# Weight products of a hybrid encoder layer: 512 columns and two token groups at a time, in place of 256 columns and one

## The chip, the cores and the metric

The kernel runs on one core of one Trainium2 chip. The metric is the device time of one launch in microseconds (us). The core's engines are named as in the profile: PE is the matrix engine and PEld its load of the stationary operand, DVE the vector engine, ACT the scalar engine, POOL the GpSimd engine, SP the engine that issues most transfers. L321 is line 321 of the kernel.

## The reference

One encoder layer for two sequences, `x_prompt` of 512 tokens (g = 0 in the kernel) and `x_sample` of 1024 tokens (g = 1), width 1024, all in float32. Gated linear attention with eight heads (A) and retention with eight heads (R) run side by side over the same projection `u @ w_in`; their outputs are mixed by gates and go through the last product, `w_out`.

```python
ada = jax.nn.silu(c) @ w_ada + b_ada
shift, scale, gate = jnp.split(ada, 3, axis=-1)
u = x * (1 + scale[:, None, :]) + shift[:, None, :]
proj = u @ w_in                                       # [T, 7168 + 1024]
aq, af_f, af_b, ai, ag, rq, rk, rv, rg = jnp.split(proj, IN_OFFSETS, axis=-1)
...
o_a = _hgrn2_dir(q_a, k_f, logf_f, v_a) + _flip(_hgrn2_dir(...))
y_a = (_rms_norm(o_a) * a_norm_w).reshape(B_, T, A_WV) * jax.nn.silu(ag.astype(F32))
q_r = _apply_rope(rq ..., cos, sin) * R_DK ** -0.5
k_r = _apply_rope(rk ..., cos, sin)
o_r = _layer_norm(_retention_dir(q_r, k_r, v_r, lg[0]) + _flip(_retention_dir(...)))
y_r = (o_r.reshape(B_, T, R_WV) * jax.nn.silu(rg.astype(F32))).astype(dt)
p_a = y_a @ w_pa
p_r = y_r @ w_pb
g_a, g_r = jnp.split(jax.nn.sigmoid(u @ w_mg + b_mg), 2, axis=-1)
s = (g_a * p_a + g_r * p_r) @ w_out
h = DEEPNORM_ALPHA * x + (1 + gate[:, None, :]) * s
return (_layer_norm(h) * ln_g + ln_b).astype(dt)
```

## The kernel before

**Products.** Every large product is exact: both operands are split into a high and a low F32R part, and three matmuls per slice of 128 of the contraction (high by low, low by high, high by high) are added up in a PSUM bank. `gemm_f` holds weight columns stationary and moves 512 tokens (L310). `gemm_t` holds 128 tokens stationary and moves 256 weight columns (L321); its outputs have tokens on the partitions. Both are generators: they yield after every 12 matmuls of 256 columns, or 6 of 512.

**Weights.** `Stream` holds the weights in their order of use. A piece of 512 KB is loaded into one of two raw buffers, ACT writes its high part (L94), DVE its low part (L103; POOL in the last product of g = 0), and both stand in a ring of four slots until the product has used them. A piece of 128 columns takes one slot; for `gemm_t` two pieces take two slots and give 256 columns.

**Banks.** The large products share three PSUM banks (`gbank`, tile name `g`), the attention stages have three others (`l`) and two (`t`). A bank is free for its next use when ACT or DVE has read the last result out of it. Two token groups of 256 columns fill one bank, and their read-out (the evacuation) is emitted behind the second.

**Order.** The program is scheduled by hand: the order in which the code emits instructions is each engine's order. `interleave` (L129) draws on a generator of matmuls, the filler, and at each yield emits, where they are due, the split of the next weight piece and attention stages (`Stage`); the code behind a yield, such as an evacuation, follows behind them. The sequence g = 0 has units A0 to A3, then R0 and R1, each of two heads (lanes). While the stages of a unit run, the filler is `mid` of the same unit (A: values and output gates; R: values, then gates) and `pre` of the next (A: queries and forget gates by `gemm_f`; R: queries and keys, rotated). Then come the gate products and blocks of 512 tokens (one for g = 0, two for g = 1, which are the last two), each with `pblock` (`w_pa`, `w_pb`, by `gemm_f`) and `oblock` (`w_out`, by `gemm_t`). In `oblock`, `epi` (L933) evacuates a bank (L937), adds the residual (L940) and takes statistics (L941); `finish` (L911) normalises a row of 128 tokens and stores it. In the last block, it is emitted right behind the last `epi` of its row. While `oblock` of g = 0 runs, stages transpose and scale the tokens of g = 1 (L1004, L1009, L1015).

```python
while i < len(stages):
    ...
    th = s.w * max(left + credit, 0.0) / max(weight, 1e-9)
    if credit < th:
        break
    ...
    s.fn()
```

The functions that the diff touches, with their lines:

Of the kernel before, what the change touches and what calls it, by code (L numbers as in the profile page):

```python
# [25 lines left out]
class Stream:  # L26
    """The weights in order of use: raw pieces are loaded, split into two F32R parts, used, released."""
# [28 lines left out]
    def open(self, j):  # L56
        """the slots of a piece, if they are free"""
        kind, ps = self.todo[j]
        need = 2 if kind == "t" else 1
        if self.used + need > self.ring:  # L60
            return False
        self.used += need
        if kind == "t":
            h = self.w_pool.tile([128, NK, 256], F32R, name="wh", tag="w", bufs=self.ring)
            l = self.w_pool.tile([128, NK, 256], F32R, name="wl", tag="w", bufs=self.ring)
            self.tiles[j] = (h, l)
            self.parts = [(h[:, :, 128 * i:128 * i + 128], l[:, :, 128 * i:128 * i + 128]) for i in range(2)]
        else:
            shape = [128, 2, 768] if kind == "k" else [128, 2, NK, 128]
# [59 lines left out]
def interleave(filler, total, stages, marks, ws, lead=0.0):  # L129
    """Emit the filler's steps with the stages spread between them, after a lead, and the weights' splits."""  # L130
# [32 lines left out]
def layer(ctx, tc, x_p, x_s, c_p, c_s, w_ada, b_ada, w_in, hgrn_lb, a_norm_w, ret_decay, w_pa, w_pb, w_mg, b_mg,  # L163
# [86 lines left out]
    def order_pre(u):  # L250
        if u.kind == "A":
            for ls in u.wl:
                h = u.lanes[ls[0]][0]
                for seg in range(3):
                    ws.add("f", (w_in, 1024 * seg + 128 * h))
        else:
# [4 lines left out]
    def order_mid(u):  # L261
        if u.kind == "A":
# [16 lines left out]
    for g in range(2):  # L279
# [15 lines left out]
        for b in range(NT[g] // 512):  # L295
            for part, n in p_order:
                ws.add("f", ((w_pa, w_pb)[part], 128 * n))
            for n in range(4):
                ws.add("t", (w_out, 256 * n), (w_out, 256 * n + 128))
# [5 lines left out]
    def gemm_f(ps, w, a):  # L305
        """ps[n, t] += sum_k w[k, n] a[k, t]; a: (hi, lo) as lists of [128, 512] over k"""
# [9 lines left out]
    def gemm_t(ps, w, a, t0, k0=0, k1=NK):  # L316
        """ps[t, n] += sum_k a[k, t] w[k, n]"""
# [9 lines left out]

    def u_f(g, b):
# [49 lines left out]

    def mid_A(u):
# [26 lines left out]
    def update(u, l, h):  # L406
        """decays of blocks of h become those of blocks of 2h"""
# [174 lines left out]
    def pre_R(u):  # L582
        u.X, u.Vt, u.Gt, u.St, u.C = {}, {}, {}, {}, {}
        for ls in u.wl:
            j, w = ws.get()
            for l in ls:
                b = u.lanes[l][1]
                X = u.X[l] = sb("X", [128, 4, 384])
                for c in range(0, 4, 2):
# [3 lines left out]
                    for e in range(2):  # L593
                        r = 4 * b + c + e
                        t = sb("sg", [128, 2, 256])
                        a = ps[:, e, 0:1]
                        sw = bass.AP(a.tensor, a.offset + 32, [list(a.ap[0]), [64, 4], [-32, 2], [1, 32]])
                        cos = rope[:, r, 0:1, :].to_broadcast([128, 4, 64])
                        sin = rope[:, r, 1:2, :].rearrange("p o (a b) -> p o a b", a=2).to_broadcast([128, 4, 2, 32])
                        V.tensor_tensor(out=t[:, 0, :].rearrange("p (a b) -> p a b", a=4),  # L600
                                        in0=ps[:, e, :].rearrange("p (a b) -> p a b", a=4), in1=cos, op=ALU.mult)
                        V.tensor_tensor(out=t[:, 1, :].rearrange("p (a b c) -> p a b c", a=4, b=2), in0=sw, in1=sin,
                                        op=ALU.mult)
                        tq = [t[:, i, 0:128].rearrange("p (a o b) -> p a o b", a=2, o=1).to_broadcast([128, 2, 2, 64])
                              for i in range(2)]
                        G.tensor_tensor(out=X[:, c + e, 0:256].rearrange("p (a o b) -> p a o b", a=2, o=2),
                                        in0=tq[0], in1=tq[1], op=ALU.add)
                        G.tensor_tensor(out=X[:, c + e, 256:384], in0=t[:, 0, 128:256], in1=t[:, 1, 128:256],
                                        op=ALU.add)
# [231 lines left out]
    yb = {}  # L841

    def load_y(g, b, part):
        """the loads of a part's two halves, in four pieces"""
# [61 lines left out]
    def oblock(g, b, st, last):  # L906
        hs, gt, lg, lb = st["h"], bc["gt"], bc["lg"], bc["lb"]
        ap_s = [lambda k, t0, p=p: st["s"][k // 4][p][:, k % 4, t0:t0 + 128] for p in range(2)]
        stat = cp.tile([128, 4, 28], F32, name="stat", tag="stat")

        def finish(i):  # L911
            def fn():
                h, ss = hs[i], stat[:, i]
                V.bn_aggr(ss[:, 24:26], ss[:, 0:24].rearrange("p (a b) -> p a b", a=4))  # L914
                G.tensor_scalar(out=ss[:, 26:27], in0=ss[:, 25:26], scalar1=EPS, scalar2=None, op0=ALU.add)  # L915
                G.tensor_tensor(out=ss[:, 27:28], in0=ss[:, 26:27], in1=nhalf[:, 0:1], op=ALU.pow)
                for q in range(2):
                    hq = h[:, 512 * q:512 * q + 512]
                    V.scalar_tensor_tensor(out=hq, in0=hq, scalar=ss[:, 24:25], in1=lg[q], op0=ALU.subtract,
                                           op1=ALU.mult)  # L920
                t0 = 512 * b + 128 * i
                for q in range(2):
                    hq = h[:, 512 * q:512 * q + 512]
                    if q == 0 or (last and i == 3):
                        V.scalar_tensor_tensor(out=hq, in0=hq, scalar=ss[:, 27:28], in1=lb[q], op0=ALU.mult,
                                               op1=ALU.add)
                    else:
                        S.activation(out=hq, in_=hq, func=AF.Copy, scale=ss[:, 27:28])
# [4 lines left out]
        def epi(n, i, ps):  # L933
            m = ps.shape[1]
            t = sb("sg", [128, m, 256])
            gg = gt[n // 2][:, 256 * (n % 2):256 * (n % 2) + 256].rearrange("p (o c) -> p o c", o=1)
            V.tensor_tensor(out=t, in0=ps, in1=gg.to_broadcast([128, m, 256]), op=ALU.mult)  # L937
            for e in range(m):
                h = hs[i + e][:, 256 * n:256 * n + 256]
                V.scalar_tensor_tensor(out=h, in0=h, scalar=ALPHA, in1=t[:, e, :], op0=ALU.mult, op1=ALU.add)  # L940
                V.bn_stats(stat[:, i + e, 6 * n:6 * n + 6], h)  # L941

        ws_n = {}

        def part(n, i, step, left):
            if n not in ws_n:
                ws_n[n] = ws.get()
            j, w = ws_n[n]
            ps = gbank([128, step, 256])
            for e in range(step):  # L950
                yield from gemm_t(ps[:, e, :], w, ap_s, 128 * (i + e))
            epi(n, i, ps)
            if not left:
                ws.done(j)

        # the last rows of s come last
        ws_n[0] = ws.get()
        banks = [gbank([128, 1, 256]) for _ in range(2)]
        for k0, k1 in ((0, NK - 1), (NK - 1, NK)):
            for e in range(2):  # L960
                yield from gemm_t(banks[e][:, 0, :], ws_n[0][1], ap_s, 128 * e, k0, k1)
        for e in range(2):
            epi(0, e, banks[e])
        order = [(0, 2, 1), (0, 3, 1), (1, 0, 2), (1, 2, 2), (2, 0, 2)]
        if last:
            order += [(3, 0, 1), (3, 1, 1), (2, 2, 1), (3, 2, 1), (2, 3, 1), (3, 3, 1)]
        else:
            order += [(2, 2, 2), (3, 0, 2), (3, 2, 2)]
        for x, (n, i, step) in enumerate(order):
            yield from part(n, i, step, any(m == n for m, _, _ in order[x + 1:]))  # L970
            if last and n == 3:
                finish(i)()
        st["finish"] = [] if last else [Stage(finish(i)) for i in range(4)]

# [44 lines left out]
    def u_parts():  # L1019
        """the next part of each product of u_stage that still lacks one"""  # L1020
# [6 lines left out]
    def ada_mm(ps, w):  # L1027
        """silu(c) times columns of w_ada: four sums over k, rows 32 j and 32 j + 1 of ps"""
# [4 lines left out]
    def ada_out(ps, row, jobs):  # L1033
        """the sum of the four, with the columns on the partitions, plus a bias and a constant"""
# [6 lines left out]
    def startup():  # L1041
# [47 lines left out]
        # silu(c) = c / (1 + exp(-c))  # L1089
# [12 lines left out]
        def bounds():  # L1102
# [3 lines left out]
            # softmax over the one layer, its cumulative sum less its first row  # L1106
# [11 lines left out]
        def log_sigmoids():  # L1118
            # lg = log_sigmoid(r) = min(r, 0) - log1p(e), e = exp(-|r|); log1p(e) = 2 atanh(z), z = e / (2 + e)
# [107 lines left out]
    def pre(u):  # L1227
        return pre_A(u) if u.kind == "A" else pre_R(u)

    def mid(u):  # L1230
        return mid_A(u) if u.kind == "A" else mid_R(u)
# [96 lines left out]
```

## Time and profile before

| | |
|---|---|
| time, median of 3 runs | 2136.13 us (2135.5 to 2137.14) |
| span of the profiled execution, first to last instruction | 2135.2 us |
| mean granted clock of the matrix engine in it | 0.998 of full speed |
| PE busy | 2108.5 us, 99% of the span |
| DVE, ACT, POOL busy | 53%, 35%, 20% |
| chain that ended last: PE's share | 95% |
| of it `gemm_f` (L310) and `gemm_t` (L321) | 41% and 38% |

The profile is of one execution; what lies around its span is 0.9 us to the median of the runs. The chain that ended last is followed back from the last instruction, at each step to what released it. Matrix products are pipelined, and the end of one is modelled, so that the time of a run of them is read from their starts, not from the length of one.

### The profile page before, as it was taken

Reading aid. Unit: us, or ns where it says so; the run is one execution under the profiler, and the core shown is the slowest. Engines: PE = TensorE matmul, PEld = TensorE weight load, DVE = VectorE, ACT = ScalarE, POOL = GpSimd, SP = SyncE. Lnnn points to the kernel's source line nnn. Section 1 sums busy time; section 2 is a strip of 40 time slices with the busy share of each in tenths; the row PEclk is TensorE's granted clock in tenths of the full one; section 3 lists DMA queues with packets and bytes.
Section 4 is the critical chain, followed back from the end, with each engine's and each line's share of the span. In section 5 each row is a group of like instructions: output and inputs, shape, how many; then the busy total and the mean of one; then the engine's idle time right before and its main releaser. Section 6 shows DMA issues by size and latency. Waiting matters only on the chain.

```text
span 2135.2 us, 45792 instructions
## 1 busy us (share of the span) xinstructions
PE 2108.5 (99%) x19331; PEld 1892.8 (89%) x19331; DVE 1122.3 (53%) x2242; ACT 746.7 (35%) x1570; POOL 437.7 (20%) x668
## 2 busy tenths in 40 slices
PE   7999999999999999999999999999999999999997
PEld 5898899998888988899889889999999888889887
DVE  4856764644334965554565457353543442245657
ACT  3644553223322534444444435212121233322221
POOL 3322233321000332121121214332322100000101
PEclk9999999999999999999999999999999999999999
DMA  9322323246776421111111211212212256577752
GB/s 285 111 84 85 92 85 106 70 129 187 226 243 201 140 80 61 41 50 61 41 61 41 70 31 61 65 41 65 85 40 85 84 163 211 185 234 225 242 184 80
DMA packets 340205, 247.29 MB, mean 116 GB/s; under 512 B 9564, under 2 KB 303680, under 8 KB 338976
## 3 DMA queue, kind: packets, MB, share of 16 engines
q1 hardware_dynamic: 332112, 229.75, 34.9%
q10 hardware_dynamic: 6944, 12.59, 1.5%
q8 instruction: 152, 2.49, 0.5%
q0 software_dynamic: 944, 2.02, 0.3%
q14 instruction: 53, 0.43, 0.1%
HBM read 199.23 MB, written 45.10 MB: 114 GB/s over the span
## 4 chain that ended last, share of the span: by engine, by line
PE 95%; DMA 1%; DVE 1%; POOL 1%; issue 1%; ACT 1%; SPq 0%; POOLq 0%; DVEq 0%; ACTq 0%
PE g L310 41%; PE g L321 38%; PE l L542 2%; PE l L430 2%; PE t L505 2%; PE l L459 1%; PE l L742 1%; PE l L740 1%; PE t L677 1%; PE g L1171 1%; PE t L489 1%; PE l L1171 1%; PE t L707 1%; PE l L725 1%; PE t L1031 1%
## 5 line engine op out<-in xcount | busy, mean ns | idle before, releaser
L321 PE MATMUL g<-wh,u 128*128 128x256 f32 x3840 | 736.2, 287 | 0.0
L310 PE MATMUL g<-u,w 128*128 128x512 f32 x2736 | 671.7, 397 | 0.0
L321 PEld LDWEIGHTS g<-wh,u 128*128 128x128 f32 x3840 | 609.5, 191 | 8.9 <-issue 4.0
L310 PEld LDWEIGHTS g<-u,w 128*128 128x128 f32 x2736 | 499.7, 188 | 100.7 <-issue 1.2
L321 PE MATMUL g<-wl,u 128*128 128x256 f32 x1920 | 542.6, 283 | 0.0
L321 PEld LDWEIGHTS g<-wl,u 128*128 128x128 f32 x1920 | 367.1, 191 | 0.1
L103 DVE TENSOR_TENSOR w<-raw,w 128x1024 fp32r<-128x1024 f32 (+1 forms) x144 | 174.8, 1215 | 209.6 <-ACT w L94 209.5
L310 PE MATMUL g<-y,w 128*128 128x512 f32 x1152 | 261.8, 389 | 0.0
L310 PEld LDWEIGHTS g<-y,w 128*128 128x128 f32 x1152 | 216.1, 188 | 44.9
L414 DVE TENSOR_TENSOR X<-X,T 128x512 f32<-128x512 f32 x336 | 219.1, 698 | 22.2 <-issue 20.4
L94 ACT ACTIVATE w<-raw 128x1024 fp32r<-128x1024 f32 (+1 forms) x146 | 151.5, 1047 | 138.9 <-DMA raw<-in_w_pb 36.4
L103 DVE TENSOR_TENSOR wl<-raw,wh 128x1024 fp32r<-128x1024 f32 x98 | 122.6, 1262 | 104.2 <-ACT wh L94 104.2
L416 POOL TENSOR_TENSOR T<-T 128x512 f32<-128x512 f32 (+6 forms) x168 | 119.7, 739 | 83.6 <-DVE T L343 81.6
L94 ACT ACTIVATE wh<-raw 128x1024 fp32r<-128x1024 f32 x104 | 106.8, 1055 | 38.2 <-PE g L321 33.7
L321 PE MATMUL g<-wh,sl 128*128 128x256 f32 x384 | 109.0, 284 | 0.0
L446 POOL COPY A<-D 32x128 f32<-32x128 f32 x96 | 57.4, 598 | 248.4 <-DVE D L439 245.4
L321 PE MATMUL g<-wl,sh 128*128 128x256 f32 x384 | 107.6, 280 | 0.0
L321 PE MATMUL g<-wh,sh 128*128 128x256 f32 x384 | 107.6, 280 | 0.0
L403 ACT ACTIVATE KM<-X 128x256 f32<-128x256 f32 x120 | 51.5, 430 | 126.2 <-DVE X L414 122.5
L915 POOL TENSOR_SCALAR stat<-stat 128x1 f32<-128x1 f32 x12 | 9.2, 765 | 373.7 <-DVE stat L914 373.7
L826 ACT ACTIVATE sg<-g,vec 128x512 f32<-128x512 f32 x48 | 33.0, 687 | 127.2 <-PE g L310 127.2
L321 PEld LDWEIGHTS g<-wl,sh 128*128 128x128 f32 x384 | 73.3, 191 | 0.1
(197 smaller groups left out, 2390.7 us busy)
## 6 DMA issues: line engine op xcount, KB each, us to landing
raw<-in_w_in SPq DMA_DIRECT2D x122, 512.0 KB, 4.1
yd<-yT SPq DMA_DIRECT2D x96, 256.0 KB, 2.1
raw<-in_w_mg SPq DMA_DIRECT2D x48, 512.0 KB, 3.9
y<-yd SPq DMA_DIRECT2D x24, 1024.0 KB, 8.9
gd<-sg ACTq DMA_DIRECT2D x48, 256.0 KB, 2.7
raw<-in_w_pa SPq DMA_DIRECT2D x24, 512.0 KB, 4.7
raw<-in_w_pb SPq DMA_DIRECT2D x24, 512.0 KB, 4.0
gt<-gd SPq DMA_DIRECT2D x48, 256.0 KB, 4.7
```

Source lines behind the costliest of these rows:

```text
L94: self.nc.scalar.activation(out=hi, in_=raw, func=AF.Copy)
L103: self.lo.tensor_tensor(out=lo, in0=raw, in1=hi.bitcast(F32), op=ALU.subtract)
L310: T.matmul(ps, w[wi][:, k, :], a[ai](k), start=n == 0, stop=n == 3 * NK - 1)
L321: T.matmul(ps, a[ai](k, t0), w[wi][:, k, :], start=k == 0 and n == 0, stop=k == NK - 1 and ai == wi)
L403: S.activation(out=K4[:, :, 0, :], in_=halves(u.X[l][:, 0, :], h)[:, :, 0, :], func=AF.Copy)
L414: V.tensor_tensor(out=v, in0=v, in1=f, op=ALU.mult)
L416: G.tensor_tensor(out=T2, in0=Tv[:, :, :, 0], in1=Tv[:, :, :, 1], op=ALU.mult)
L430: T.matmul(ps[32 * i:32 * i + 32, c, :], km[:, c0:c0 + 32], qq, start=True, stop=True, tile_position=(0, 32 * i))
L446: G.tensor_copy(out=A[32 * i:32 * i + 32, :, 32 * i:32 * i + 32], in_=u.Dt[l][32 * i:32 * i + 32, :, :])
L505: T.matmul(ps[:, m, :], kt[:, m, :], u.Vt[l][:, c, :], start=True, stop=True)
L542: T.matmul(ps[:, c, :], a, b, start=i == 0, stop=i == len(mm) - 1)
L1171: T.matmul(acc[l, seg], w[wi][:, n0:n0 + 128], uh[0, 0, ai][:, k, :], start=k == 0 and n == 0, stop=k == 7 and n == 2)
```

## The change

Three products of g = 0 (`mid` of an A unit, `pre` and `mid` of an R unit) and `oblock` of all three blocks no longer use `gemm_t` but a new `gemm_q`. Its moving operand is 512 weight columns. A weight piece is now two slices of the contraction by 512 columns, again 512 KB and one slot; four of them are the whole product's columns. One pass over the four pieces accumulates two groups of 128 tokens side by side in two banks, and a second pass over the same four pieces does the other two groups; a slot is released in the second pass. Both banks are evacuated behind the pass. The units of g = 1 keep `gemm_t`. A raw piece is loaded by 4 transfers (`pre` of R), 2 (`mid` of A) or 1. In the last block's second half the token groups go (0, 1), then 2, then 3. `epi` works on 512 columns, and statistics have two entries a row in place of four. Comments and docstrings were removed, so that line numbers move.

```diff
+        elif kind == "q":
+            raw = raw.rearrange("p (a k) n -> p a (k n)", a=2)
...
+        if isinstance(c0, tuple):
+            q, cols = c0
+            tq = t.rearrange("p (a k) n -> p a (k n)", a=2)
+            w = 512 // len(cols)
+            for x, c in enumerate(cols):
+                nc.sync.dma_start(tq[:, :, w * x:w * x + w], src[256 * q:256 * q + 256, c:c + w].rearrange(
+                    "(k p) n -> p k n", p=128))
+            return
...
+    def add_q(src, *cols):
+
+        for q in range(4):
+            ws.add("q", (src, (q, cols)))
...
+    def gemm_q(rows, a, evac):
+
+        tiles = []
+        for x, group in enumerate(rows):
+            banks = [gbank([128, 512]) for _ in group]
+            for q in range(4):
+                if x == 0:
+                    tiles.append(ws.get())
+                w = tiles[q][1]
+                for t0, ps in zip(group, banks):
+                    for k in (2 * q, 2 * q + 1):
+                        for wi, ai in ((0, 1), (1, 0), (0, 0)):
+                            T.matmul(ps, a[ai](k, t0), w[wi][:, k - 2 * q, :], start=k == 0 and ai == 1,
+                                     stop=k == NK - 1 and ai == wi)
+                    yield 6 * 0.218
+                if x == len(rows) - 1:
+                    ws.done(tiles[q][0])
+            for t0, ps in zip(group, banks):
+                evac(t0, ps)
+
+    PAIRS = ((0, 128), (256, 384))
...
+        def evac(t0, ps):
+            c = t0 // 128
+            for l in range(2):
+                S.activation(out=u.Vt[l][:, c, :], in_=ps[:, 128 * l:128 * l + 128], func=AF.Copy)
+            t = sb("sg", [128, 256])
+            S.activation(out=t, in_=ps[:, 256:512], func=AF.Sigmoid)
+            for l in range(2):
+                V.tensor_tensor(out=u.Gt[l][:, c, :], in0=ps[:, 256 + 128 * l:384 + 128 * l],
+                                in1=t[:, 128 * l:128 * l + 128], op=ALU.mult)
+
+        yield from gemm_q(PAIRS, u_t(0, 0), evac)
...
+            for l in range(2):
+                rotate(u.X[l], ps[:, 256 * l:256 * l + 256], t0 // 128, t0 // 128)
...
+            if last and n == 1:
                 finish(i)()
+
+        for n in range(2):
+            yield from gemm_q(((0, 128), (256,), (384,)) if last and n else PAIRS, ap_s,
+                              lambda t0, ps, n=n: epi(n, t0 // 128, ps))
```

How the change moves instructions is read from the order in which each engine gets them. The first place is PE in unit A1, where the first pair of token groups ends and the second begins. `l<-X,KM` are the products of an attention stage; `g_753` is the second bank of the first pair, `g_918` and `g_919` are the two of the next. Before, one bank follows another:

```order
L321 MATMUL g_806<-wl_685,u_153 128x256
L321 MATMUL g_806<-wh_684,u_153 128x256
L321 MATMUL g_806<-wh_684,u_154 128x256
L321 MATMUL g_806<-wl_685,u_153 128x256
L321 MATMUL g_806<-wh_684,u_153 128x256
L430 MATMUL l_902<-X_712,KM_841 32x32 [waits Activation_49]
L430 MATMUL l_902<-X_712,KM_841 32x32 x15
L430 MATMUL l_927<-X_728,KM_863 32x32 [waits DVE_49,PE_49,Activation_49]
L430 MATMUL l_927<-X_728,KM_863 32x32 x15
L321 MATMUL g_958<-wh_771,u_154 128x256
```

Now:

```order
L364 MATMUL g_753<-w_783,u_154 128x512
L364 MATMUL g_753<-w_783,u_153 128x512 x2
L494 MATMUL l_856<-X_716,KM_813 32x32 [waits Activation_49]
L494 MATMUL l_856<-X_716,KM_813 32x32 x15
L494 MATMUL l_881<-X_732,KM_835 32x32 [waits PE_49,Activation_49]
L494 MATMUL l_881<-X_732,KM_835 32x32 x15
L364 MATMUL g_918<-w_686,u_154 128x512
L364 MATMUL g_918<-w_686,u_153 128x512 x2
L364 MATMUL g_918<-w_686,u_154 128x512
L364 MATMUL g_918<-w_686,u_153 128x512 x2
L364 MATMUL g_919<-w_686,u_154 128x512 [waits DVE_49,PE_49,Activation_49]
L364 MATMUL g_919<-w_686,u_153 128x512 x2
```

The stage stands at the end of the pass, and six matmuls into the next pass a matmul waits for DVE and ACT: its bank is the one that the first token group of the pass before filled.

The second place is ACT at the same point: the mixes of that stage (`KM`) and the evacuation behind them. Before:

```order
L403 ACTIVATE KM<-X 128x128x2 [waits DVE_49,PE_49,Activation_49]
L404 ACTIVATE KM<-X 128x128x2 [waits DVE_49]
L403 ACTIVATE KM<-X 128x128x2 [waits DVE_49,PE_49,Activation_49]
L404 ACTIVATE KM<-X 128x128x2 [waits DVE_49]
L390 ACTIVATE V<-g 128x256
L392 ACTIVATE sg<-g 128x256
```

Now:

```order
L467 ACTIVATE KM<-X 128x128x2 [waits DVE_49,PE_49,Activation_49]
L468 ACTIVATE KM<-X 128x128x2 [waits DVE_49]
L467 ACTIVATE KM<-X 128x128x2 [waits DVE_49,PE_49,Activation_49]
L468 ACTIVATE KM<-X 128x128x2 [waits DVE_49]
L433 ACTIVATE V<-g 128x128 x2
L435 ACTIVATE sg<-g 128x256
L433 ACTIVATE V<-g 128x128 x2
L435 ACTIVATE sg<-g 128x256
```

In both, the evacuation stands behind the four mixes of the stage; now it is that of two banks.

The third place is DVE where `pre` of R0 ends, among the last stages of A3: `yT<-t,vec,yT` is the output stage of each lane of A3, and `sg<-g,rope` are the rotations that evacuate a bank of R0. Before:

```order
L548 TENSOR_TENSOR y<-l,G 128x512 [waits Activation_49] x2
L572 SCALAR_TENSOR_TENSOR yT<-t,vec,yT 128x512 [waits DMAHW0_49,Activation_49]
L572 SCALAR_TENSOR_TENSOR yT<-t,vec,yT 128x512 [waits DMAHW2_49,Activation_49]
L600 TENSOR_TENSOR sg<-g,rope 128x256 [waits Pool_49]
L602 TENSOR_TENSOR sg<-g,rope 128x256
L600 TENSOR_TENSOR sg<-g,rope 128x256 [waits Pool_49]
L602 TENSOR_TENSOR sg<-g,rope 128x256
```

Now:

```order
L636 SCALAR_TENSOR_TENSOR yT<-t,vec,yT 128x512 [waits Activation_49]
L105 TENSOR_TENSOR w<-raw,w 128x1024 [waits DMAHW3_49]
L636 SCALAR_TENSOR_TENSOR yT<-t,vec,yT 128x512 [waits DMAHW6_49,Activation_49]
L653 TENSOR_TENSOR sg<-g,rope 128x256 [waits Pool_49]
L655 TENSOR_TENSOR sg<-g,rope 128x256
L653 TENSOR_TENSOR sg<-g,rope 128x256 [waits Pool_49]
L655 TENSOR_TENSOR sg<-g,rope 128x256
L653 TENSOR_TENSOR sg<-g,rope 128x256 [waits DVE_49,Pool_49]
L655 TENSOR_TENSOR sg<-g,rope 128x256
L653 TENSOR_TENSOR sg<-g,rope 128x256 [waits DVE_49,Pool_49]
L655 TENSOR_TENSOR sg<-g,rope 128x256
```

The rotations of two banks stand behind the second output stage, eight of them in place of four, and a weight split (L105) stands between the two output stages.

## Rows read from the trace of the kernel before

**Rows 1.** The profile's page: busy time, share of the span, instructions.

```profile
PE 2108.5 (99%) x19331; PEld 1892.8 (89%) x19331; DVE 1122.3 (53%) x2242; ACT 746.7 (35%) x1570; POOL 437.7 (20%) x668
```

**Rows 2.** Waits of PE: total, times, longest, us; the largest, and another engine's.

```profile
PE t L1031 <- DMA wa<-in_w_ada: 6.9, 2, 3.7
...
PE l L430 <- ACT KM L404: 0.5, 2, 0.3
```

**Rows 3.** Chain that ended last, its longest pieces: start us, us, what, instructions.

```profile
348.79 25.91 PE g L321 x216
...
1748.94 197.22 PE g L310 x870
1946.16 45.23 PE g L321 x384
```

**Rows 4.** The same chain from 65 to 110 us.

```profile
73.44 4.50 PE g L321 x36
...
97.90 4.33 PE g L310 x18
```

**Rows 5.** Timeline, 72 to 84 us: start, us, engine, line, operation, idle before.

```profile
73.21 0.28 ACT L434 ACTIVATE D<-l 128x128 f32<-128x128 f32 x1 [1.21 <-PE l L430]
...
77.87 0.89 PE L430 MATMUL l<-X,KM 128*32 128x32 f32 x64
...
78.69 0.39 PE L321 MATMUL g<-wh,u 128*128 128x256 f32 x1
...
81.50 0.44 ACT L404 ACTIVATE KM<-X 128x256 f32<-128x256 f32 x1
...
81.84 0.37 ACT L390 ACTIVATE V<-g 128x256 f32<-128x256 f32 x1
...
82.10 0.38 ACT L392 ACTIVATE sg<-g 128x256 f32<-128x256 f32 x1
...
82.52 0.42 DVE L393 TENSOR_TENSOR G<-g,sg 128x256 f32<-128x256 f32 x1 [1.04 <-ACT sg L392]
```

**Rows 6.** Timeline, 338 to 357 us.

```profile
347.59 1.20 PE L566 MATMUL t<-ident,y 128*128 128x128 f32 x4
...
351.11 0.69 ACT L571 ACTIVATE yT<-t,vec 128x512 fp32r<-128x512 f32 x1 [2.12 <-DMA yd<-yT]
...
351.90 0.75 DVE L572 SCALAR_TENSOR_TENSOR yT<-t,vec,yT 128x512 fp32r<-128x512 f32 x1 [2.13 <-DMA yd<-yT]
...
352.56 0.41 DVE L600 TENSOR_TENSOR sg<-g,rope 128x256 f32<-128x256 f32 x1
...
352.89 0.41 DVE L602 TENSOR_TENSOR sg<-g,rope 128x256 f32<-128x256 f32 x1
```

**Rows 7.** Timeline of DVE in `oblock` of g = 0.

```profile
717.80 1.36 DVE L1009 TENSOR_SCALAR q<-l,sc,shf 128x128 f32<-128x128 f32 x4 [0.98 <-PE l L1004]
719.22 0.69 DVE L937 TENSOR_TENSOR sg<-g,gt 128x512 f32<-128x512 f32 x1
719.94 0.43 DVE L940 SCALAR_TENSOR_TENSOR h<-h,sg 128x256 f32<-128x256 f32 x1
```

**Rows 8.** Timeline of PE's last product and of DVE in the tail.

```profile
2123.40 0.28 PE L321 MATMUL g<-wh,sh 128*128 128x256 f32 x1
...
2125.59 1.22 DVE L940 SCALAR_TENSOR_TENSOR h<-h,sg 128x256 f32<-128x256 f32 x1
...
2128.55 0.26 DVE L914 BATCH_NORM_AGGREGATE stat<-stat 128x2 f32<-128x24 f32 x1
2128.85 1.41 DVE L919 SCALAR_TENSOR_TENSOR h<-h,stat,lg 128x512 f32<-128x512 f32 x2
2130.72 1.42 DVE L925 SCALAR_TENSOR_TENSOR h<-h,stat,lb 128x512 f32<-128x512 f32 x2 [0.46 <-POOL stat L916]
```

**Rows 9.** Groups by line and form: busy us, mean ns of one.

```profile
L103 DVE TENSOR_TENSOR w<-raw,w 128x1024 fp32r<-128x1024 f32 x136 | 167.1, 1230 | 198.5 <-ACT w L94 198.4
L94 ACT ACTIVATE w<-raw 128x1024 fp32r<-128x1024 f32 x138 | 144.8, 1059 | 135.4 <-DMA raw<-in_w_pb 36.4 <-PE g L321 20.9 <-ACT sg L826 19.0
```

More of the change, by code (lines that the diff above doesn't have):

```diff
@@ L297, in layer @@
                 ws.add("f", ((w_pa, w_pb)[part], 128 * n))
-            for n in range(4):
-                ws.add("t", (w_out, 256 * n), (w_out, 256 * n + 128))
+            for n in range(2):
+                add_q(w_out, 512 * n)
     marks = set()
@@ L579, in stages_A, with rotate, pre_R0, evac @@
         return st
+    def rotate(X, ps, r, c):
+        t = sb("sg", [128, 2, 256])
+        a = ps[:, 0:1]
+        sw = bass.AP(a.tensor, a.offset + 32, [list(a.ap[0]), [64, 4], [-32, 2], [1, 32]])
+        cos = rope[:, r, 0:1, :].to_broadcast([128, 4, 64])
+        sin = rope[:, r, 1:2, :].rearrange("p o (a b) -> p o a b", a=2).to_broadcast([128, 4, 2, 32])
+        V.tensor_tensor(out=t[:, 0, :].rearrange("p (a b) -> p a b", a=4),
+                        in0=ps.rearrange("p (a b) -> p a b", a=4), in1=cos, op=ALU.mult)
+        V.tensor_tensor(out=t[:, 1, :].rearrange("p (a b c) -> p a b c", a=4, b=2), in0=sw, in1=sin, op=ALU.mult)
+        tq = [t[:, i, 0:128].rearrange("p (a o b) -> p a o b", a=2, o=1).to_broadcast([128, 2, 2, 64])
+              for i in range(2)]
+        G.tensor_tensor(out=X[:, c, 0:256].rearrange("p (a o b) -> p a o b", a=2, o=2), in0=tq[0], in1=tq[1],
+                        op=ALU.add)
+        G.tensor_tensor(out=X[:, c, 256:384], in0=t[:, 0, 128:256], in1=t[:, 1, 128:256], op=ALU.add)
+    def pre_R0(u):
+        u.X, u.Vt, u.Gt, u.St, u.C = {}, {}, {}, {}, {}
+        for l in range(2):
+            u.X[l] = sb("X", [128, 4, 384])
+        def evac(t0, ps):
+            for l in range(2):
+                rotate(u.X[l], ps[:, 256 * l:256 * l + 256], t0 // 128, t0 // 128)
+        yield from gemm_q(PAIRS, u_t(0, 0), evac)
+    def mid_R0(u):
+        for l in range(2):
+            u.Vt[l] = sb("T1", [128, 4, 256])
+        def evac_v(t0, ps):
+            for l in range(2):
+                S.activation(out=u.Vt[l][:, t0 // 128, :], in_=ps[:, 256 * l:256 * l + 256], func=AF.Copy)
+        def evac_g(t0, ps):
+            c = t0 // 128
+            t = sb("sg", [128, 512])
+            S.activation(out=t, in_=ps, func=AF.Sigmoid)
+            for l in range(2):
+                if c % 2 == 0:
+                    u.Gt[l, c // 2] = sb("T2" if l == 0 else "G", [128, 2, 256])
+                V.tensor_tensor(out=u.Gt[l, c // 2][:, c % 2, :], in0=ps[:, 256 * l:256 * l + 256],
+                                in1=t[:, 256 * l:256 * l + 256], op=ALU.mult)
+                if c % 2:
+                    marks.add((u, "g", l, c // 2))
+        yield from gemm_q(PAIRS, u_t(0, 0), evac_v)
+        marks.add((u, "v"))
+        yield from gemm_q(PAIRS, u_t(0, 0), evac_g)
     def pre_R(u):
@@ L593, in pre_R @@
                     for e in range(2):
[L594 to L609, printed above, removed]
+                        rotate(X, ps[:, e, :], 4 * b + c + e, c + e)
             ws.done(j)
@@ L933, in epi @@
         def epi(n, i, ps):
[L934 to L971, printed above, removed]
+            t = sb("sg", [128, 512])
+            V.tensor_tensor(out=t, in0=ps, in1=gt[n], op=ALU.mult)
+            h = hs[i][:, 512 * n:512 * n + 512]
+            V.scalar_tensor_tensor(out=h, in0=h, scalar=ALPHA, in1=t, op0=ALU.mult, op1=ALU.add)
+            V.bn_stats(stat[:, i, 6 * n:6 * n + 6], h)
+            if last and n == 1:
                 finish(i)()
+        for n in range(2):
+            yield from gemm_q(((0, 128), (256,), (384,)) if last and n else PAIRS, ap_s,
+                              lambda t0, ps, n=n: epi(n, t0 // 128, ps))
         st["finish"] = [] if last else [Stage(finish(i)) for i in range(4)]
```

37 lines of the change are left out of this document (26 added, 11 removed).

## Prediction

> **What bounds the kernel now.** I read the page first. PE is busy 99% of the span and DVE, the next, 53% [rows 1]; the chain of work that ended last lies on PE for 95%. So the time is PE's work plus what PE waits for, plus a short tail. Next came PE's waits by engine and line. The largest are for loads at the start, and of the other engines' results ACT's mixes head the list with 0.5 us in the whole run [rows 2]. No wait for a bank of the large products is in that list. Two consequences follow: a saving in PE's issue comes out in full, and any new wait of PE comes out in full too. The third view was the chain's long pieces, which give PE's pace in each form of product; the last were the timelines around the places where the change moves evacuations.
>
> **The gain on PE.** The change replaces 1920 matmuls of 256 columns in the units of g = 0 by 960 of 512, and 1152 in the three output blocks by 576. The columns are as many; what is saved is what a matmul costs beside its columns. For the units, two uninterrupted pieces of different length give it: 216 matmuls take 25.91 us [rows 3] and 36 take 4.50 [rows 4], so one is (25.91 - 4.50) / 180 = 0.1189 us, with 0.22 us once per piece. In the output block, 384 in one piece take 45.23, 0.1178 each. A matmul of 512 columns in `gemm_f` is 197.22 / 870 = 0.2267 [rows 3]; its piece of 18 takes 4.33 [rows 4], which leaves 0.25 once. I take these for `gemm_q`, which has the same sizes, though which operand is stationary differs. A pair of old ones for a new one then saves 2 x 0.1189 - 0.2267 = 0.0111 us in the units and 0.0089 in the blocks: 960 x 0.0111 + 576 x 0.0089 = 10.7 + 5.1 = 15.8 us. Stages break the new product into 77 pieces, as many as before; each costs 0.03 more at its start, 2.4 in all. **Gain 13.4 us**, between 11 and 16.
>
> [...] The rows show 9 to 11 ns a pair.
>
> **The price: a bank that is needed too soon.** There are still three banks, and a pass now holds two. A pass takes the free third bank for its first token group and, for its second, the bank that the first group of the pass before filled. PE gets to it after six matmuls, 1.36 us behind the start of the pass. Before, a bank was wanted again two banks, some 11 us, after it was full, which is why an evacuation up to 6 us late cost nothing. That evacuation is emitted behind the whole pass, and behind any stage or split that falls due at its last yield. Where nothing stands there, it starts as the bank's last matmul ends, 1.36 us before the pass ends, and has 2.7 us: enough for two copies, a sigmoid and two products. Where a stage stands there, it is late. I went through the boundaries in the order of the new kernel:
>
> - *A0, A1, A2, between the passes.* A stage stands exactly there. Its products run on PE from 77.87 to 78.76; ACT does its four mixes and is free at 81.84, when the evacuation begins [rows 5]. The new one for the bank that is wanted needs two copies of 128 columns (0.28 each, as the ACT instruction at 73.21) and a sigmoid of 0.38, to 82.8, then two products on DVE. One of 256 columns takes 0.42 [rows 5]; I estimate 0.3 for each of 128 and end at 83.3. PE is there at 78.76 + 1.36 + 0.05 = 80.2. So 3.1 us each (2.5 to 3.5), 9.3 together.
> - *A3, between the passes:* its stage lies some steps earlier; 0.6.
> - *The end of `pre` of R0's first pass:* a stage of A3 and a weight split (1.23, [rows 9]) stand ahead of the rotations on DVE. 2 to 3.9, I take 3.
> - *From `pre` to `mid` of R0.* The output stage of A3's second lane stands ahead. Its transposes end at 347.59 + 1.20 = 348.79. DVE's part waits for ACT at 351.11, which waits for the store of the lane before, and ends at 352.56, where the rotations begin. The four of the wanted bank, 0.33 from start to start (352.56, 352.89), end at 353.9 [rows 6]. PE wants the bank at 348.79 + 1.36 + 0.05 = 350.2. So 3.7 (3 to 4).
> - *Other boundaries of R0 and R1:* five have stages or splits near, 0 to 1.4 each, 2 in all. The value passes are read by two ACT copies and cost nothing.
> - *`oblock` of g = 0:* at two boundaries the scaling of the tokens of g = 1 stands ahead on DVE, 1.36 us [rows 7], ahead of an evacuation of 0.69. About 1 each, 2. The two blocks of g = 1 have few stages there: nothing.
>
> Sum 20.6 us; with each at its ends 14 to 25.
>
> **The tail.** The last matmul starts at 2123.40 now, 11.8 us before the end [rows 8]. The old order spreads the four rows' last evacuations, so that three rows are done by then. In the new one rows 0 and 1 end their product together, 48 x 0.2267 = 10.9 us before the end of the last; rows 2 and 3 follow 5.4 us apart. Per row, DVE has the gate product 0.69 [rows 7], the residual and the statistics at 0.71 each (estimated as half of the pair of 1.42 on 512 columns), 0.26 + 1.41, a wait for POOL of 0.46 and another 0.71 [rows 8]: 4.95, and 5.66 for the last row, where DVE does both halves. From 10.6 before the end, rows 0 to 2 keep it until 4.3 behind it, the last row until 9.9; the store takes 3.1 as now (2132.1 to the span's 2135.2). That is 13.0 against 11.8, or 1.2 more. Where POOL works beside it, a DVE instruction of 0.43 [rows 7] took 1.22 [rows 8]; 0.8 more in three rows is 3.6. I take 2.4.
>
> **Edits costed at nothing.** Evacuations have twice as many small instructions for values and gates of A, on engines with half of their time free. Weight pieces are as large as before; ACT and DVE split one in 1.06 + 1.23 us [rows 9], and DVE and ACT work on different ones. A slot is given back every 12 matmuls of the second pass, 2.7 us, which is longer than a split. The more numerous transfers move the same bytes. If this cover is gone, it is the second rival below.
>
> **Sum.** 20.6 + 2.4 - 13.4 = +9.6 us on a span of 2135.2: 2144.8. The median of the runs lies 0.9 above that span, so **2145.7 us**. A difference under 0.2%, 4.3 us, can't be told from none: the bounds are 2131.9 and 2140.4.
>
> **Rivals.**
> 1. *The evacuations come in time.* ACT and DVE are over 45% idle, and the stage ahead could be through sooner: with PE delayed by one wait, the mixes' inputs from DVE have had longer to be ready. If the stages cost the passes nothing, 13.4 - 2.4 = 11 us are gained: 2125. Against it: the mixes at 77.87 wait for products that PE makes in the same stage, so that a delay of PE delays them as well. It decides for faster from the point where all waits for banks sum to less than 6.7 us (13.4 - 2.4 - 4.3).
> 2. *Weights come late.* All four slots are held until the second pass gives them back, and the next product's four splits can only begin then. If the first piece is late by one split of 2.3 us at each of the 16 products (4 of A, 6 of R, 6 of the blocks), that is 37 us, 2183; half of it is 2164. Against it: the split is shorter than the interval at which slots come free, and PE waited for none so far [rows 2].
> [...]
> 4. *Some of the waits are shorter,* because the stage stands a step away from the pass's end in the run of things: 12 us of waits in place of 20.6 gives 2137, no difference that can be told.
>
> **Chances.** The forecast, waits of 14 to 25 us, has 0.68; rival 1 0.11; rival 2 0.06; rival 3 0.04; rival 4 0.11. The forecast's own ends are 2139 (2136.1 + 14 + 2.4 - 13.4) and 2154 (2136.1 + 25 + 3.6 - 11). The range 2131 to 2154 takes in rival 4 and leaves out rival 1, and rivals 2 and 3 for the most part. Faster by over 0.2%: 0.12. Within 0.2%: rival 4 and the low end of the forecast, 0.18. Slower: 0.70.
>
> **What the profile would show.** If I am right: PE's waits list the new matmul line, some 3 us at a time, for the products on DVE behind the sigmoid of A and for the rotations of R, 18 to 23 us in all, nearly all before 500 us; pieces of the new product at 0.2267 a matmul in the chain; and a tail of 13 to 15 us behind the last matmul with DVE at work throughout. [...] What would make it wrong most easily is the boundary estimate of 3.1: it counts three times, and rests on one stage's timeline.

## The result, and the profile after

The changed kernel takes 2173.35 us (median of 4 runs, 2171.76 to 2175.16) against 2136.64 for the kernel before (4 runs, 2135.5 to 2137.7): a ratio of 1.0174, 95% interval 1.016 to 1.0189. It is slower by 36.7 us; the forecast was 9.6 us slower, and the time lies 19 us above the range. The span of the profiled execution is 2171.8.

The page of the changed kernel, where its first part answers to [rows 1]:

```profile
span 2171.8 us, 42817 instructions
...
PE 2113.5 (97%) x17795; PEld 1816.8 (84%) x17795; DVE 1115.5 (51%) x2209; ACT 749.0 (34%) x1594; POOL 428.9 (20%) x668
```

PE has 1536 instructions fewer and is busy 5.0 us longer, in a span of 36.6 us more. So there are two losses: 31.6 us in which PE stands still, and PE's own work, which should have shrunk by 13.4.

PE's waits (engine, line, what it waited for: us in total, times, longest), which answer to [rows 2]:

```profile
PE g L364 <- ACT sg L435: 9.4, 4, 2.9
...
PE g L364 <- DVE sg L655: 5.8, 3, 3.9
PE g L364 <- DVE G L437: 4.5, 1, 4.5
PE l L523 <- DVE X L478: 3.8, 6, 1.0
...
PE l L494 <- ACT KM L468: 2.5, 9, 0.4
PE g L364 <- DVE w L105: 2.5, 1, 2.5
...
PE g L364 <- DVE G L688: 0.9, 2, 0.7
PE g L364 <- DVE sg L1035: 0.7, 1, 0.7
```

The lines that read a bank (L435, L655, L437, L688, L1035) sum to 21.3 us: the waits for banks that the forecast put at 20.6. Beside them there are 2.5 us for a weight split in A0, and 6.3 for the stages' updates (L478) and mixes (L468), of which 0.5 were there before.

One of these waits in the timeline, at the place of [rows 5], between the two passes of A0; the last row is from A3, for comparison:

```profile
81.51 0.89 PE L494 MATMUL l<-X,KM 128*32 128x32 f32 x64
...
82.33 1.66 PE L364 MATMUL g<-w,u 128*128 128x512 f32 x6
...
85.15 0.43 ACT L468 ACTIVATE KM<-X 128x256 f32<-128x256 f32 x1
...
85.80 0.38 ACT L435 ACTIVATE sg<-g 128x256 f32<-128x256 f32 x1
...
86.21 1.10 DVE L437 TENSOR_TENSOR G<-g,sg 128x128 f32<-128x128 f32 x4 [1.10 <-ACT sg L435]
...
86.85 4.58 PE L364 MATMUL g<-w,u 128*128 128x512 f32 x12 [2.86 <-ACT sg L435]
...
333.69 3.04 PE L364 MATMUL g<-w,u 128*128 128x512 f32 x12
```

The stage stands at the end of the pass, PE does six matmuls of the next and stands still until 86.85, since ACT does the stage's mixes to 85.5 before it comes to the bank. The last row also holds what the forecast has no term for: 12 matmuls of 512 columns take 4.58 us there, where 12 take 3.04 in A3. The granted clock says why. Windows of the changed kernel, the first over all units of g = 0 and the gate products behind them, the rest around this wait (from:to and length, PE's busy time and instructions, granted clock, DMA share, GB/s):

```profile
66.83:632.15 565.32, 534.83 (x4547) 0.98 0.36 111
...
78.00:82.00 4.00, 4.00 (x61) 1.00 0.55 165
82.00:86.00 4.00, 1.99 (x44) 1.00 0.00 0
...
88.00:90.00 2.00, 2.00 (x6) 0.50 0.00 0
90.00:92.00 2.00, 2.00 (x68) 0.75 0.00 0
92.00:96.00 4.00, 4.00 (x31) 1.00 0.01 4
```

PE stands still from about 84 to 86.85; from 87.5 to 91 its clock is granted at 0.50, and then at 1.00 again. From 87.64 to 89.77 five matmuls start 0.427 us apart, against 0.227 in long pieces at a granted clock of 1.00, so that 3.4 us filled with matmuls at half clock cost 1.6 us. In half-microsecond windows up to the last product there are five such places, at the waits of A0, A1, A2, A3 and R0 that are 2.9 to 4.5 us long (87.5, 166.0, 244.5, 343.5, 384.5), one of them twice as long as the others. They last 20.5 us together, PE is busy for 19.8 of them, and at the two paces that costs 9.3 us. Before the change there is none between the start and the last product.

The same stretch of the program before the change, in one window:

```profile
65.56:598.18 532.62, 531.42 (x5506) 1.00 0.39 117
```

The units of g = 0 take 32.7 us more, 565.3 against 532.6, of which PE stands still for 29.3 (30.5 against 1.2). Its busy time rises by 3.4, and less the 9.3 that half clock costs it falls by 5.9.

The longest pieces of the chain, which answer to [rows 3] (an output block's whole product, all its passes, in one piece, and most of the last block's):

```profile
1982.37 44.80 PE g L364 x192
...
2114.23 32.21 PE g L364 x138
```

The blocks' new product takes 44.80 / 192 = 0.2333 us a matmul, not 0.2267, against 2 x 0.1178 for a pair before. And the tail, which answers to [rows 8]:

```profile
2158.40 0.63 PE L364 MATMUL g<-w,sh 128*128 128x512 f32 x2
...
2163.21 1.22 DVE L1037 SCALAR_TENSOR_TENSOR h<-h,sg 128x512 f32<-128x512 f32 x1
...
2167.31 1.42 DVE L1025 SCALAR_TENSOR_TENSOR h<-h,stat,lb 128x512 f32<-128x512 f32 x2 [0.46 <-POOL stat L1016]
```

The last matmul starts at 2158.63 (the second of the first row), 13.2 us before the end, where it was 11.8.

### The profile page after: what moved, and what is told of

Read it like the earlier page. It is cut to its first block, busy times and chain, and to the rows that moved or that the text cites. A ratio compares the mean times of both kernels' runs of the same rounds, so it can differ in the third digit from the quotient of the medians.

```text
span 2171.8 us, 42817 instructions
## 1 busy us (share of the span) xinstructions
PE 2113.5 (97%) x17795; PEld 1816.8 (84%) x17795; DVE 1115.5 (51%) x2209; ACT 749.0 (34%) x1594; POOL 428.9 (20%) x668
## 4 chain that ended last, share of the span: by engine, by line
PE 80%; DVE 2%; POOL 1%; issue 1%; DMA 0%; ACT 0%; POOLq 0%; DVEq 0%; SPq 0%; ACTq 0%
PE g L334 37%; PE g L345 22%; PE g L364 10%; PE l L606 2%; PE l L494 2%; PE t L569 1%; PE l L842 1%; PE l L840 1%; PE t L777 1%; PE l L523 1%; PE l L825 1%; PE t L807 1%; PE t L553 1%; PE t L873 0%; PE t L630 0%
## 5 line engine op out<-in xcount | busy, mean ns | idle before, releaser
L345 PE MATMUL g<-wh,u 128*128 128x256 f32 x2560 | 491.9, 287 | 0.0
L345 PEld LDWEIGHTS g<-wh,u 128*128 128x128 f32 x2560 | 406.6, 191 | 6.2 <-issue 2.7
L105 DVE TENSOR_TENSOR w<-raw,w 128x1024 fp32r<-128x1024 f32 (+1 forms) x202 | 245.5, 1217 | 263.1 <-ACT w L96 263.0
L345 PE MATMUL g<-wl,u 128*128 128x256 f32 x1280 | 361.7, 283 | 0.0
L364 PE MATMUL g<-w,u 128*128 128x512 f32 x960 | 245.5, 408 | 23.0 <-ACT sg L435 9.4
L345 PEld LDWEIGHTS g<-wl,u 128*128 128x128 f32 x1280 | 244.8, 191 | 0.0
L364 PEld LDWEIGHTS g<-w,u 128*128 128x128 f32 x960 | 180.8, 194 | 66.4 <-issue 13.7
L478 DVE TENSOR_TENSOR X<-X,T 128x512 f32<-128x512 f32 x336 | 219.7, 701 | 28.2 <-issue 21.7
L364 PE MATMUL g<-w,sh 128*128 128x512 f32 x384 | 120.7, 395 | 0.0
L364 PEld LDWEIGHTS g<-w,sh 128*128 128x128 f32 x384 | 72.2, 188 | 16.6
L105 DVE TENSOR_TENSOR wl<-raw,wh 128x1024 fp32r<-128x1024 f32 x40 | 50.4, 1267 | 65.1 <-ACT wh L96 65.1
L364 PE MATMUL g<-w,sl 128*128 128x512 f32 x192 | 77.4, 403 | 0.7 <-DVE sg L1035 0.7
```

Of the source, the lines that this page charges most:

```text
L105: self.lo.tensor_tensor(out=lo, in0=raw, in1=hi.bitcast(F32), op=ALU.subtract)
L345: T.matmul(ps, a[ai](k, t0), w[wi][:, k, :], start=k == 0 and n == 0, stop=k == NK - 1 and ai == wi)
L364: T.matmul(ps, a[ai](k, t0), w[wi][:, k - 2 * q, :], start=k == 0 and ai == 1, stop=k == NK - 1 and ai == wi)
L478: V.tensor_tensor(out=v, in0=v, in1=f, op=ALU.mult)
```

## The experiments

**Theory W.** A pass wants its second bank too soon; PE waits, and behind each wait of some 3 us it works at half clock for a while. Rivals: the weights come late (L), the time only moves to the stages (S), 512 columns are slow in themselves (P), and for the clock, that something else in the units lowers it.

**Which part of the change.** Two kernels with half of the change each: the units alone (the old `oblock` and its pieces of `w_out` put back), and the blocks alone (the old orders and functions of the units).

```diff
-            for n in range(2):
-                add_q(w_out, 512 * n)
+            for n in range(4):
+                ws.add("t", (w_out, 256 * n), (w_out, 256 * n + 128))
...
```

> The change in the units of g = 0 alone, output blocks as before. By the two traces 34 of the 36.6 us arise ahead of the first pblock: 2167 to 2173. If the blocks' tail and waits mattered as I forecast (2.4 and 2, against a gain of 5), the blocks alone would gain and this kernel would be slower than the change, 2174 to 2176.

Measured 2168.91 us, ratio 1.0155 (1.014 to 1.0171), 32.9 above the 2136.03 of before beside it.

```diff
...
-        if u.kind == "A":
-            return (mid_A if u.g else mid_A0)(u)
-        return (mid_R if u.g else mid_R0)(u)
+        return mid_A(u) if u.kind == "A" else mid_R(u)
```

> The change in the output blocks alone, units as before. By the two traces the blocks cost 1.3 in g = 0, save 0.4 in each of the others, and the tail costs 1.2: 2137 to 2140 against 2136.6, no half-clock stretch. By the forecast's own terms (gain 5.1, waits 2, tail 2.4): 2136.

Measured 2139.1 us, ratio 1.0013 (1.0004 to 1.0023), 3.1 above. The halves add up to 36.0. The loss is in the units; in the blocks the change costs a little, where my terms had it even.

**The bank waits.** Each bank is evacuated right behind its own last matmul:

```diff
+                    if q == 3:
+                        evac(t0, ps)
                     yield 6 * 0.218
...
-            for t0, ps in zip(group, banks):
-                evac(t0, ps)
```

> The changed kernel, with each bank evacuated right behind its own last matmul, ahead of the stage or split that falls due at the same yield. Theory W (the second bank of a pass is wanted 1.36 us into the pass, and its evacuation stands behind a stage; and each such wait of some 3 us is followed by a stretch at half of the granted clock): the 21 us of waits for DVE and ACT at the new matmul line fall to under 5, the five half-clock stretches go (10 us), time 2136 to 2146 against 2173. Rival S (the evacuations only change places with the stages, whose products PE then waits for): time above 2155, waits at the attention products' lines. Rival P (512 columns themselves are slow): no change, 2170.

Measured 2151.45 us, ratio 1.0071 (1.0056 to 1.0086): 21.9 less than the change, but not the 2136 to 2146 of theory W. PE's waits in this kernel:

```profile
PE l L494 <- ACT KM L468: 7.7, 12, 0.9
...
PE t L1076 <- DMA xt<-in_x_sample: 3.4, 1, 3.4
...
PE l L523 <- DVE X L478: 3.0, 2, 1.9
PE g L364 <- DVE w L105: 2.5, 1, 2.5
PE g L334 <- DVE u L1087: 1.5, 1, 1.5
```

All waits for banks are gone, and three half-clock stretches are left (at 73, 329 and 725 us), which cost 4.8 us. Rival P, no change, is out. Rival S is right in part: PE now waits 7.7 us for the stages' mixes, where the change has 2.5. The evacuation of the second bank, which nobody wants yet, now stands ahead of a stage; whether that makes these waits is asked below.

The same by another way, an order of groups that leaves time for the bank:

```diff
-    PAIRS = ((0, 128), (256, 384))
+    PAIRS = ((0, 128), (256,), (384,))
```

> The changed kernel with token groups (0, 1), then 2, then 3 everywhere, so that the bank which group 3 wants has been full for 5.4 us and the next product finds free banks; weights are given back in the last 24 matmuls, 1.36 us apart in place of 2.7. Theory W: bank waits under 5 us, no half-clock stretch, 2136 to 2146. Rival L (weights late, since splits of 2.3 us a piece can't follow slots that come free 1.36 us apart): waits at the new line for the splits of 10 us and more, above 2150.

Measured 2161.97 us, ratio 1.0121 (1.0104 to 1.0138). No wait for a bank is left here either, but this one appears, and at it three half-clock stretches, two of which begin while PE still stands (PE is busy in them for 12.8 us, which costs 6.0):

```profile
PE g L364 <- DVE w L105: 15.3, 8, 6.0
```

Rival L holds for this order: the four pieces of a product are given back within its last 5.4 us.

**Only the bank that is wanted.** The first bank early, the second behind the pass as in the change:

```diff
+                    if q == 3 and t0 != group[-1]:
+                        evac(t0, ps)
                     yield 6 * 0.218
...
+            evac(group[-1], banks[-1])
```

> The changed kernel with only the first bank of a pass evacuated early (behind its own last matmul, ahead of the last two yields), the second bank behind the pass as in the change. The second bank is wanted one whole pass later and can stand behind the stage. If the 10 us of waits for the stages' mixes in the kernel that evacuates both early come from the second bank's evacuation ahead of a stage: they fall to about 3, and the time is 2141 to 2147 against 2151.5. If they come from the faster or denser order of stages itself: 2150 to 2153.

Measured 2144.63 us, ratio 1.0035 (1.0021 to 1.0048), as forecast in time, not in detail: the waits for mixes fall from 7.7 to 4.9, those for updates rise from 3.0 to 4.2. So moving the second bank's evacuation takes away only 1.6 us of these waits. The rest of the 6.8 us gained lies elsewhere: a wait for the tokens of g = 1 falls from 3.4 to 1.5, the half-clock stretch behind it goes (1.6), and so does the wait of 1.5 for `u` (L1087). That the time came out as forecast is in part luck.

With A0 and the blocks as before the change (`mid_A` for the first unit, the old `oblock`):

```diff
-        if u.g == 0:
+        if u.g == 0 and u is not us[0]:
             h = u.lanes[0][0]
...
-            return (mid_A if u.g else mid_A0)(u)
+            return (mid_A if u.g or u.i == 0 else mid_A0)(u)
...
```

> The same early evacuation of the first bank, with the first A unit and the three output blocks left as before the change. That takes away A0's wait for a weight split (2.5 and a half-clock stretch of 1.7) and the blocks' loss (3 and more). With the units' gain of some 5 us on PE: 2132 to 2138, about the kernel before; above 2140 if the stages' waits remain.

Measured 2137.51 us, ratio 1.0005 (0.9997 to 1.0014): in the profiled execution no half-clock stretch, no bank wait, and no gain. The window over the units is

```profile
64.95:597.68 532.73, 523.66 (x4643) 1.00 0.39 117
```

PE is busy for 7.8 us less than before the change, and stands still for 7.9 more (9.1 against 1.2). The gain on PE is there (864 new matmuls save 9.6 at the prediction's pace, less their restarts), and waits take it all. The timeline shows what PE waits for in A1, where the second pass has ended at 164.9:

```profile
165.09 0.49 DVE L438 TENSOR_TENSOR G<-g,sg 128x128 f32<-128x128 f32 x2 [1.09 <-ACT sg L436]
...
166.04 1.22 DVE L105 TENSOR_TENSOR w<-raw,w 128x1024 fp32r<-128x1024 f32 x1 [0.46 <-ACT w L96]
...
167.18 0.29 DVE L504 COPY_PREDICATED D<-mask,l 128x128 f32<-128x128 uint8 x1
...
169.22 0.46 PE L495 MATMUL l<-X,KM 128*32 128x32 f32 x32
...
170.57 0.46 PE L495 MATMUL l<-X,KM 128*32 128x32 f32 x32 [0.89 <-ACT KM L469]
```

A split of 1.22 us on DVE stands ahead of the stage's mask and updates. Hence the next kernel, in which `interleave` emits splits behind the stages of a yield:

```diff
-        if since >= 2.5 and ws.tick():
-            since = 0.0
-        elif since >= 1.2:
-            ws.flush()
         while i < len(stages):
...
             s.fn()
             i += 1
+        if since >= 2.5 and ws.tick():
+            since = 0.0
+        elif since >= 1.2:
+            ws.flush()
```

> The kernel with first bank early, A0 and blocks as before (2137.5 us), and the weight splits emitted behind the stages of a yield in place of ahead of them, in the whole program. In that kernel PE still waits 7.5 us for the mixes and updates of the A units' stages, and in the trace a split of 1.23 us on DVE stands ahead of the updates that those mixes need. If the split's place makes these waits: they fall to under 3 us, and the time is 2131 to 2135. If they come from the stages' own density: the waits stay at 7, time 2136 to 2139. If the later splits make the weights late: waits for the splits at the new line, above 2140.

Measured 2134.46 us, ratio 0.9989 (0.998 to 0.9998). The stages' waits fall from 7.5 to 3.4:

```profile
PE l L495 <- ACT KM L469: 2.7, 6, 0.9
...
PE l L524 <- DVE X L479: 0.7, 2, 0.4
PE g L364 <- DVE w L105: 0.4, 1, 0.4
```

So the splits' place made more than half of them, if not as much as forecast; the units of g = 1, where the order changed as well, take the same time (1207.7 us). The profiled execution is the slowest of the ten (2137.9 us): in it PE waits 2.0 us for the tokens of g = 1, with a half-clock stretch behind it.

**The R units alone,** with the first bank early (the edit is against the kernel with A0 and the blocks as before; the splits are back in their place):

```diff
-        if u.g == 0 and u is not us[0]:
+        if u.g == 0 and u.kind == "R":
...
-            return (mid_A if u.g or u.i == 0 else mid_A0)(u)
+            return mid_A(u)
```

> The change in the R units alone, with the first bank of a pass evacuated early; A units and output blocks as before the change. In the kernel with both kinds of units changed, the waits of PE that are left (7.5 us) all lie in the A units, and R has none at its banks. 576 new matmuls save 6.4 us less the restarts of 50 pieces at 0.03, 1.5: 2130 to 2133, faster than before by about 0.2%. If the R units' gain is eaten by waits that I haven't seen: 2135 to 2138.

Measured 2131.92 us, ratio 0.9978 (0.9969 to 0.9987) against 2136.55 of before in the same series. The new line is not among PE's waits at all; behind the loads at the start they begin with

```profile
PE l L495 <- ACT KM L469: 0.5, 2, 0.3
```

as before the change. This is the fastest of the twelve kernels, 4.6 us below the one before: where nothing is paid for it, the saving that I worked out from the rows is there (4.9). With A1 to A3 changed as well, and nothing else, the time was 5.6 us longer (2137.51), so that the A units did not pay in any of these kernels.

**The clock by itself.** The kernel before, with seven waits put into the last `pblock`:

```diff
+            if g == 1 and b == 1 and i in WAIT:
+                z = sb("sg", [128, 512], name="z")
+                for x in range(WAIT[i]):
+                    S.activation(out=z, in_=z if x else t, func=AF.Copy)
+                zt = tbank([128, 128])
+                T.transpose(zt, z[:, 0:128], ident)
...
+    WAIT = {1: 1, 3: 2, 5: 3, 7: 4, 9: 5, 11: 6, 13: 8}
```

> The kernel before, with seven waits of PE put into the last pblock, where PE has run without a break: behind seven of the sixteen products a transpose on PE waits for 1, 2, 3, 4, 5, 6 or 8 ACT copies of 128x512 in a row, about 1.5 to 6 us (0.7 for the evacuation and 0.6 a copy), 25 us together. Theory C (a wait of PE of some 3 us is by itself followed by a stretch at half of the granted clock): the trace shows a half-clock stretch of about 3.5 us behind the longer ones and none behind the shortest, and the time is above before by the waits and 1.7 us for each stretch, 30 to 35 us in all. Rival (the stretches in the changed kernel come from something else in the units, such as the attention products of 32 columns): no stretch here, time above before by the waits alone, about 25.

Measured 2179.71 us, ratio 1.0204 (1.019 to 1.0218), 43.4 above. The waits sum to more than I had put, 30.2 us in seven (in three of them DVE ends a row of the block before, ahead of the evacuation that the first copy reads); windows around the first three:

```profile
2003.00:2007.00 4.00, 0.50 (x3) 1.00 0.64 200
2008.00:2011.00 3.00, 3.00 (x8) 0.50 0.60 202
2012.00:2019.00 7.00, 7.00 (x32) 1.00 0.33 100
2022.00:2032.00 10.00, 10.00 (x45) 1.00 0.41 127
2033.00:2037.00 4.00, 0.25 (x2) 1.00 0.61 197
2039.00:2041.50 2.50, 2.50 (x7) 0.50 0.30 80
```

Behind the first wait, 3.6 us, the clock is at 0.50; behind the second, 2.1 us (to 2022.0), it stays at 1.00; behind the third, 4.4, it falls again, and so at the other four, once for twice as long. In the six stretches PE is busy for 21.2 us (the last two begin well before the wait is over), which costs 10.0 at the paces of 0.427 and 0.227; 30.2 + 10.0 is 40.2 of the 43.4, and the rest is left for the seven transposes and restarts. Theory C holds in a kernel where nothing else was touched: without the half clock it would have been some 33.

**The pace.** The last block's stationary operand is read from other tiles:

```diff
+        if last:
+            ap_s = [lambda k, t0, p=p: yb[1][p][:, k, t0:t0 + 128] for p in range(2)]
```

> The changed kernel, with the last output block's stationary operand read from the tiles of y in place of those of s (so that this block multiplies other numbers by w_out). In the changed kernel that block goes at 0.2333 us a matmul, while the same product with u stationary settles at 0.2267. If the tile that the stationary operand lies in decides: 0.2267 here, 0.6 us less. If the place in the program (behind a wait, two banks side by side) decides: 0.2333 as in the change.

Measured 2171.36 us (one run). The same piece of the chain as above is

```profile
2112.89 31.32 PE g L364 x138
```

31.32 / 138 = 0.2270 against 0.2334. The tile that the stationary operand is read from decides, or the numbers in it, which changed along with it and were not tried apart; the place in the program does not. In `mid` of R1, with u stationary, the kernel with both banks early has

```profile
446.74 27.24 PE g L364 x120
```

which is 0.227 too. What it is about the tiles of `s` that costs 0.007 us a matmul stays open; before, with 256 columns, they were the faster ones (0.1178 against 0.1189).

## Why the prediction was wrong

The direction and the mechanism of the bank waits were right; the size was not. The largest step that failed is one sentence of the first part: "any new wait of PE comes out in full too". Five waits, of 2.9 to 4.5 us, came out at more than their length, since half clock followed them: 9.3 us for which the sum has no term. Two more steps failed. Under "Edits costed at nothing" the splits and the fuller evacuations were put at nothing, and PE waited 8.3 us for a split, mixes and updates. And "Gain 13.4 us" came out at 6.3. Without the half clock the time would still be 2164, above the range of 2131 to 2154; only without all three would it lie inside. By steps (us, in the profiled executions; the last but one is what is left):

| step | forecast | measured |
|---|---|---|
| PE's gain in the units | -8.9 | -5.9 |
| PE's gain in the blocks | -4.5 | -0.4 |
| waits for banks | 20.6 | 21.3 |
| wait for a weight split in A0 | 0 | 2.5 |
| waits for the stages' mixes and updates | 0 | 5.8 |
| half clock at waits | 0 | 9.3 |
| tail | 2.4 | 1.4 |
| start, units of g = 1 and the rest | 0 | 2.6 |
| sum | 9.6 | 36.6 |

- *Waits for banks.* The sum was right, and the estimate of 3.1 us for A0 to A2 was nearly what the trace has (3.26 from start to start, less one matmul, 3.0). The parts were not: A3 between its passes has 4.5 (a stage and a split on DVE that I had put some steps earlier) in place of 0.6, and the end of `pre` of R0's first pass about 0.5 in place of 3; from `pre` to `mid` of R0 it is 3.9 against 3.7. That the sums agree, 21.3 and 20.6, is in part luck: errors of 3.9 up and 2.5 down. That the early evacuation takes all of them away shows their cause.
- *Half clock.* No rival named it. The kernel with waits put in shows it apart from everything else.
- *The gain in the units.* In the kernel with A1 to A3 and R changed and no half clock it is 7.8 us for 864 of the 960 matmuls, so the pace was right there. That PE's restarts behind the long waits take the rest in the changed kernel is likely and not shown.
- *The stages.* I went through the work that stands ahead of an evacuation, and not through what the evacuations and bunched splits stand ahead of. Holding four pieces to the second pass puts the splits next to the pass's end, which rival 2 described as late weights; what they delayed were the stages' updates, as the kernel with late splits shows.
- *The pace.* That `gemm_q` goes at another pace than `gemm_f` had a chance of 0.04 (rival 3). Where u is stationary it is the same (0.227 in long pieces, and R alone gains 4.6 us, near the 4.9 worked out for it); in the blocks it is another, and 0.2333 leaves 0.0023 us a pair. I had taken one pace for both, from a product with another stationary operand.
- *The tail* was right in kind: DVE works through it, with the slowed instruction of 1.22 us (L1037, 0.69 in the median) in it, and 1.4 us lies near the lower bound of 1.2.

What stays open: whether a fourth bank would do without any reordering (not tried; the other five banks are the stages'), and what decides whether a shorter wait is followed by half clock. The wait of 2.5 us for a split in A0 was followed by it in four of the kernels (units alone, other order of groups, both early, first early) and not in the changed one. The wait of 2.9 us for a bank in A0 was followed by it in the changed kernel and not in the one with the units alone. Two waits in A3, of 0.9 and 1.1 us close together, were followed by it in the kernel with the first bank early, and not in the next one, with A0 and the blocks as before.

## What to carry to other kernels

Before two groups share a pass, count the banks: with three, the second group of a pass waits for the first group's evacuation of the pass before, and whatever the order of emission puts ahead of that evacuation is then on PE's path. Evacuate at once the bank that is wanted next, and leave the other behind the stages. Look for a stretch at half clock behind a wait of PE, and charge the wait with it; here five waits of 2.9 to 4.5 us had one, and these stretches cost 9.3 us, nearly half as much again as the 21.3 of the waits for banks themselves.

## What was not expected of the hardware

Half clock (0.50 granted) came with five waits of 2.9 to 4.5 us in the changed kernel and with six of 3.6 to 6.1 in the kernel with waits put in, for 3.4 us at a time, and 6.8 once in each. The length of a wait alone does not tell: behind one of 2.1 us (in the kernel with waits put in) and one of 2.9 (A0, the units alone) the granted clock stayed at 1.00, and behind others of 2.0 (the late splits) and 2.5 (A0's split, in four kernels) it fell to 0.50. And one form of matmul, 128 x 128 by 512 columns, goes at 0.227 or at 0.233 us, steadily over 31 us and more, by the tile that its stationary operand is read from or the numbers in it.
